# Attention logits of a hybrid decoder layer: two heads in two halves of the matrix array, or one head at a time in the whole of it; and two loads moved

## The chip, the core and the metric

The kernel runs on one core of a Trainium2 chip. A core has five engines that run their own instruction streams in order and wait for each other by semaphores: TensorE (PE in the profile; its weight loads are PEld), VectorE (DVE), ScalarE (ACT), GpSimd (POOL) and SyncE (SP), which here only issues DMAs. The metric is the device time of one execution in microseconds; lower is better.

## What is computed

One decoder layer on 256 tokens of width 1024, all in float32. The input is projected by one matrix `w_in`; three token mixers run on the columns; their outputs are gated, merged, projected by `w_out`, normalized (LN1), and passed through a feed-forward part with a second gate from a side input `p`, and normalized again. Cut to what the change touches:

```python
sc    = einsum('bqhd,bsd->bqhs', iq, ik) * 64**-0.5        # indexer: 8 heads of 64, one key head
index = einsum('bqh,bqhs->bqs', iw, relu(sc))              # its top 64 keys are those of mixer A
logits_A = einsum('bqhd,bkd->bqhk', q, k_shared)*s + bias  # branch A: 6 heads, one key head
logits_B = einsum('bqhd,bqjhd->bqhj', q_g, k_slot)*s + bias # dilated: 4 slots x 3 groups of queries
logits_C = q @ k.T * s + bias                              # block-sparse: 6 heads, own keys
merged = sum(sigmoid(x @ Wg_b) * (o_b @ P_b) for b in 'ABC')
x = LN(alpha * x + merged @ w_out)                         # LN1, with row vectors ln1_g and ln1_b
x = LN(alpha * x + relu(x @ w_up)**2 @ w_down + sigmoid(x @ w_ple_gate) * (p @ w_ple))
```

## The kernel before

**Numbers in two parts.** Every float32 operand of a matmul is split into a high part (a rounded copy, made by ACT) and a low part (what the rounding left, made by DVE and, for early weights, POOL). A product of two such operands takes three matmuls, high by high, high by low and low by high (`prod`, L133); low by low is dropped.

**Weights.** `Weights` (L50) holds a list of units, each up to 128 x 1024. For each it issues a load on SP into one of five `raw` buffers (L71), a cast on ACT (L75) and a subtraction on DVE or DVE and POOL (L79) into one of five pairs `whi`, `wlo`. `get(i, ahead)` emits the splits up to four units past the one wanted. `W.after` names instructions behind which the next splits are held.

**The order of the work.** A planner with a model of the machine orders the instructions of each engine before the run; on the chip each engine then keeps that order. `high_priority` moves instructions up in it, `issue_after` holds one behind another, and `keep_in_program_order` pins matmuls to each other.

**Projections.** `feat(f)` (L257) computes one tile of 128 features by 256 tokens (two heads of 64) into one of three `mm` banks of PSUM with 24 matmuls of 256 columns. The first four tiles, the indexer's queries, are computed together (L403 to L408). `fill("g")` computes a tile of the gates in the same way, and `fill("c")` a tile of the branch products; they lie between the attention steps and keep PE supplied.

**Logits.** `q_pair` (L214) splits a query tile: plane 0 is its high part, plane 1 its low part, both heads above each other on 128 partitions. `k_pair` (L222) does it for keys; with two arguments it writes the same 64 rows into both halves (the indexer's key kI and branch A's key kA). `logits(q, k)` (L264) takes one query tile and gives the two heads' logits in two PSUM banks: for each block of 128 queries three products, each product for head 1 and for head 0, so 12 matmuls. Each contracts over 64 partitions, that is, uses one half of the array's rows; six have 128 columns and six have 256. There are 16 calls: 4 for the indexer (L425), 6 for the dilated pairs (`slots`, L356), 3 for the block-sparse branch (L474) and 3 for branch A (L489). DVE adds the bias to the result and takes the row extreme; ACT takes the exponential; `attend` (L308) transposes the probabilities on PE, splits them and multiplies by the values.

**Merge, `w_out`, LN1.** `merge` (L561) gates and sums the branches. `outp` multiplies by `w_out` into four banks; its last four steps go bank by bank (`finish`, L547), and `ln1` (L630) follows each bank: add the residual `PL` (L634), statistics (L611 to L618), scale and shift by the row vectors `rows1` (L623, L625), transpose on PE (L644), split (L646, L647). `PL` and `rows1`, 1 MB each, are loaded by ACT's queue behind the sixth `muls` (L601 to L603). `finish` emits splits of units ahead before it emits `ln1`: the two of `w_ple`, and the first two of `w_ple_gate` (called wpg0 and wpg1 here). L660 multiplies the side input, split in `ph` and `pl` (L464 to L467), by `w_ple`.

**The rest.** The `w_ple_gate` product, 32 tiles of `w_up` (L693, L695) and `w_down`, partly in a scheme with seven products in place of eight, follow; the change does not touch them.

Of the kernel before, what the change touches and what calls it, by code (L numbers as in the profile page):

```python
# [11 lines left out]
F32 = mybir.dt.float32  # L12
# [37 lines left out]
class Weights:  # L50


    def __init__(self, tc, raw, part):
        self.tc, self.nc = tc, tc.nc
        self.raw, self.part = raw, part
        self.units, self.done, self.parts, self.after = [], 0, {}, ()

    def add(self, src, n, hi=None, lo=None, stage=None, by="v", urgent=0):
        i = len(self.units)
# [3 lines left out]
    def _split(self, i):  # L63
        nc = self.nc
        src, n, hi, lo, r, by, _ = self.units[i]
        if callable(src):
            r = src()
        else:
            if r is None:
                r = self.raw.tile([128, 1024], F32, name="raw", tag="raw")[:, :n]  # L70
            nc.sync.dma_start(r, src)  # L71
        if hi is None:
            hi = self.part.tile([128, 1024], F32R, name="whi", tag="whi")[:, :n]
            lo = self.part.tile([128, 1024], F32R, name="wlo", tag="wlo")[:, :n]
        nc.scalar.copy(hi, r)  # L75
        cut = ((nc.vector, slice(None)),) if by == "v" else (
            (nc.vector, slice(0, by * n // 1024)), (nc.gpsimd, slice(by * n // 1024, n)))
        for e, c in cut:
            low = e.tensor_tensor(lo[:, c], r[:, c], hi[:, c].bitcast(F32), op=ALU.subtract)  # L79
            if e is nc.gpsimd:  # L80
                self.pool = low.ins
        self.parts[i] = (hi, lo)
# [13 lines left out]
def hybrid_layer(ctx: ExitStack, tc: tile.TileContext, x0, xn, pT, wqk, wva, wvb, wg, wbc, wba,  # L96
# [56 lines left out]
    pm = mid.enter_context(tc.tile_pool(name="pm", bufs=1))  # L153
    one = ctx.enter_context(ExitStack())
    right = lambda n, b: one.enter_context(tc.tile_pool(name=n, bufs=b, side="right"))
    p1, k1, kp = (right(n, b) for n, b in (("p1", 1), ("k1", 2), ("kp", 3)))

    xh = p1.tile([128, KT, S], F32R, name="xh")
    xl = p1.tile([128, KT, S], F32R, name="xl")
# [13 lines left out]
    for t in TASKS:  # L173
# [8 lines left out]
        else:  # L182
            u_q.append([add(wqk[int(t) - FIRST], 1024)])

    def toeplitz(h0, step):
        t = tp.tile([128, 3, 256], F32, name="T", tag="T")
        for i in range(3):
            nc.sync.dma_start(t[:, i], bass.AP(
                tensor=tabd.tensor,
                offset=tabd.offset + (h0 + i * step) * COPIES * N_U + 127,  # L190
                ap=[[N_U - 16, 8], [N_U - 1, 16], [1, 256]]))
        return t


# [19 lines left out]
    def q_pair(ps, scale=-0.125):  # L214

        q = qpool.tile([128, 2, S], F32R, name="q", tag="q")
        last[0] = act.mul(q[:, 0], ps, scale).ins
        low[0] = dve.scalar_tensor_tensor(q[:, 1], ps, scale, q[:, 0].bitcast(F32),
                                          op0=ALU.mult, op1=ALU.subtract).ins
        return q  # L220

    def k_pair(a, b=None):  # L222

# [79 lines left out]
            dve.tensor_tensor(V[:, b, h0:h0 + heads, DH:128], src,  # L303
                              V[:, b, h0:h0 + heads, 0:DH].bitcast(F32), op=ALU.subtract)

    n_pt = [0]

    def attend(P, vh, o, h):  # L308

        pt = pts[n_pt[0] % 2]  # L310
        n_pt[0] += 1
        t = next(ps_t)
        for c in range(3):
            pe.transpose(t[:, 128 * c:128 * c + 128], P[:, 128 * c:128 * c + 128], ident)  # L314
        act.copy(pt[:, 0], t[:, 0:384])
        dve.tensor_tensor(pt[:, 1], t[:, 0:384], pt[:, 0].bitcast(F32), op=ALU.subtract)
        v = next(ps_v).rearrange("p (a s) -> p a s", a=2)
        pe.matmul(v, lhsT=V[:, 0, vh], rhs=pt[:, :, 0:256], start=True, stop=False)  # L318
        pe.matmul(v[:, :, 128:256], lhsT=V[:, 1, vh], rhs=pt[:, :, 256:384], start=False,
                  stop=True)  # L320
        x = wk2.tile([64, 2, S], F32, name="ov", tag="ov")
        act.copy(x, v[64:128])
        dve.tensor_tensor(x, v[0:64], x, op=ALU.add)
        dve.tensor_tensor(o[64 * h:64 * h + 64], x[:, 0], x[:, 1], op=ALU.add)
# [26 lines left out]
    def slots(qs, k, Ts, vh, o):  # L351

        es = [wk2.tile([128, 3, 384], F32, name="eb", tag="eb") for _ in range(2)]
        mxs = [sm.tile([128, 2, 3], F32, name="mxb", tag="mxb") for _ in range(2)]
        for g in range(3):
            s = logits(qs[g], k)  # L356
            for h in range(2):
                for b, t in enumerate((Ts[h][:, g, 128:256], Ts[h][:, g, :])):
                    dve.tensor_tensor_reduce(es[h][:, g, QC[b]], s[h][:, QC[b]], t, op0=ALU.add,
                                             op1=ALU.min, scale=1.0, scalar=-GONE,  # L360
                                             accum_out=mxs[h][:, b, g:g + 1])
        for h in range(2):
# [23 lines left out]
    with ExitStack() as begin:  # L386
# [17 lines left out]
        for k in range(KT):  # L404
            for i, (w, x) in enumerate(((sh, xh), (sh, xl), (sl, xh))):
                for f in range(FIRST):
                    pe.matmul(first[f], lhsT=w[:, k, 128 * f:128 * f + 128], rhs=x[:, k],  # L407
                              start=k == i == 0, stop=k == KT - 1 and i == 2)  # L408
        iq = [q_pair(ps, 0.125) for ps in first]
    tp, wk, wk2, sm = (right(n, b) for n, b in (("tp", 3), ("wk", 3), ("wk2", 2), ("sm", 6)))  # L410
    with tc.issue_after(low[0]):
        dve.tensor_tensor(tab, gone, tab, op=ALU.subtract)
# [9 lines left out]

    values(u_va, 328, 0, 5, True)
    for j in range(4):
        s = logits(iq[j], kI)  # L425
        r = wk2.tile([128, 768], F32, name="ri", tag="eb")
        r = r.rearrange("p (h k) -> p h k", h=2)
        for h in range(2):
# [20 lines left out]

    for j in range(2):  # L450
        ps = feat(5 + 4 * j)
        k = k_pair(ps)
        fill("g")
        qs = []
        for g in range(3):
            qs.append(q_pair(feat(6 + 4 * j + g)))
            if g:
                fill("g")
        o = opair()
# [1 line left out]
        slots(qs, k, Ts, 1 + 2 * j, o)  # L461
        pair_out(o, 3 + j)
        fill("g")
    pr = wk2.tile([128, 2, S], F32, name="pr", tag="eb")  # L464
    nc.sync.dma_start(pr, pT)
    act.copy(ph, pr)
    dve.tensor_tensor(pl, pr, ph.bitcast(F32), op=ALU.subtract)  # L467
    values(u_vb, 384, 5, 6, False)
    fill("g")
    for j in range(3):  # L470
# [14 lines left out]
        pass  # L485
    T = None
    for j in range(3):
        q = q_pair(feat(19 + j))
        s = logits(q, kA)  # L489
        o = opair()  # L490
        for h in range(2):
            n = 2 * j + h
# [33 lines left out]
    class Wide:  # L526
# [17 lines left out]
                for c in range(len(self.cut[b])):  # L544
                    self.go(k, b, c)

        def finish(self, ks, done, spare):  # L547

            for k in ks:
                self.ws[k] = W.get(self.units[k], min(AHEAD, ks[-1] - k + spare))  # L550
            for b in range(2):
                for c in range(len(self.cut[b])):
                    for k in ks:
# [40 lines left out]
    x1 = p3.tile([128, 2, KT, 2, 128], F32R, name="x1")  # L594
    rows1 = p3.tile([128, 2, D], F32, name="rows", tag="rows")

    def row_load(t, i):
        act.dma_start(t, lnrow[i:i + 2].rearrange("r d -> (r d)").partition_broadcast(128)
                      .rearrange("p (r d) -> p r d", r=2))

    with tc.issue_after(muls[5]):  # L601
        act.dma_start(PL, xn)
        row_load(rows1, 0)  # L603

    st = {}

# [41 lines left out]
        if b == 1:  # L648
            W.after = (i0.ins, i1.ins)

    outp.finish((4, 5, 6, 7), ln1, 5)


    wp = [W.get(u, 0) for u in u_ple]
# [309 lines left out]
```

## Time and profile before

| what | value |
|---|---|
| median of 3 runs | 435.42 us (434.95 to 435.57) |
| the profiled execution, its own time | 437.98 us |
| its span, first to last instruction | 436.2 us |
| mean granted TensorE clock in it | 0.994 |
| DMA | 86.39 MB, mean 198 GB/s |

The profile is of one execution. The time of an execution holds some 1.8 us outside the span. Busy time of an engine counts its instructions' durations, overlaps once. Matmuls are pipelined: the profile shows each with a duration of some 0.28 us, but the next one starts about 0.12 us later, so what PE spends on one is read from start to start. In a timeline, a row holds the start in us, the time in us that it covers, engine, line, operation, what is written and read, shapes, the count of instructions merged into it, and in brackets an idle time before it and what ended it. The chain of waits follows the last instruction back to what released it.

### The profile page before, as it was taken

Reading aid. Unit: us, or ns where it says so; the run is one execution under the profiler, and the core shown is the slowest. Engines: PE = TensorE matmul, PEld = TensorE weight load, DVE = VectorE, ACT = ScalarE, POOL = GpSimd, SP = SyncE. Lnnn points to the kernel's source line nnn. Section 1 sums busy time; section 2 is a strip of 40 time slices with the busy share of each in tenths; the row PEclk is TensorE's granted clock in tenths of the full one; section 3 lists DMA queues with packets and bytes.
Section 4 is the critical chain, followed back from the end, with each engine's and each line's share of the span. In section 5 each row is a group of like instructions: output and inputs, shape, how many; then the busy total and the mean of one; then the engine's idle time right before and its main releaser. Section 6 shows DMA issues by size and latency. Waiting matters only on the chain.

```text
span 436.2 us, 7669 instructions
## 1 busy us (share of the span) xinstructions
PE 425.1 (97%) x2799; PEld 386.0 (88%) x2799; DVE 350.5 (80%) x625; ACT 276.2 (63%) x490; POOL 105.4 (24%) x98
## 2 busy tenths in 40 slices
PE   8999999999999999999998999999999999999993
PEld 8999999999999999999886888888888888888882
DVE  5978987577476577879957779999988897998984
ACT  6775375586787777756524567788887855665500
POOL 2563355395434566400000000000100000000001
PEclk9999999999999999999999999999999999999997
DMA  8797756457654436455960875656795377758411
GB/s 298 291 326 234 230 173 191 150 189 250 183 151 145 128 109 187 144 192 178 400 246 0 288 237 185 187 180 203 277 268 187 115 207 269 200 192 278 155 41 57
DMA packets 27690, 86.39 MB, mean 198 GB/s; under 512 B 2884, under 2 KB 6892, under 8 KB 27268
## 3 DMA queue, kind: packets, MB, share of 16 engines
q1 hardware_dynamic: 25872, 79.54, 55.1%
q0 software_dynamic: 640, 2.17, 2.9%
q10 hardware_dynamic: 1140, 4.19, 2.6%
q8 instruction: 22, 0.36, 0.3%
q14 instruction: 16, 0.13, 0.1%
HBM read 83.99 MB, written 1.90 MB: 197 GB/s over the span
## 4 chain that ended last, share of the span: by engine, by line
PE 88%; DVE 5%; issue 3%; DMA 2%; POOL 0%; POOLq 0%; ACT 0%; DVEq 0%; ACTq 0%
PE mm L136 40%; PE b L136 18%; PE mm L693 13%; PE mm L695 7%; PE b L274 3%; PE b L407 3%; DMA raw<-in_wpg_dram 2%; PE b L314 1%; PE b L318 1%; DVE hT L79 1%; DVE st L611 1%; DVE Y L625 1%; PE b L131 1%; DVE G L570 1%; DVE Y L634 1%
## 5 line engine op out<-in xcount | busy, mean ns | idle before, releaser
L79 DVE TENSOR_TENSOR wlo<-raw,whi 128x1024 fp32r<-128x1024 f32 (+5 forms) x146 | 157.5, 1092 | 41.9 <-ACT whi L75 37.9
L75 ACT CAST whi<-raw 128x1024 fp32r<-128x1024 f32 (+3 forms) x146 | 146.1, 1011 | 48.8 <-PE b L136 11.7
L79 POOL TENSOR_TENSOR wlo<-raw,whi 128x384 fp32r<-128x384 f32 (+3 forms) x58 | 78.8, 1367 | 82.6 <-ACT whi L75 73.6
L136 PE MATMUL mm<-xl,whi 128*128 128x256 f32 x336 | 95.7, 285 | 0.0
L136 PE MATMUL mm<-xh,whi 128*128 128x256 f32 x336 | 95.3, 284 | 0.0
L136 PE MATMUL mm<-xh,wlo 128*128 128x256 f32 x336 | 95.0, 283 | 0.0
L136 PEld LDWEIGHTS mm<-xl,whi 128*128 128x128 f32 x336 | 63.3, 188 | 1.0
L693 PE MATMUL mm<-x,whi 128*128 128x512 f32 x256 | 64.1, 392 | 0.0
L136 PEld LDWEIGHTS mm<-xh,whi 128*128 128x128 f32 x336 | 63.3, 188 | 0.7
L136 PEld LDWEIGHTS mm<-xh,wlo 128*128 128x128 f32 x336 | 63.3, 188 | 0.3
L693 PEld LDWEIGHTS mm<-x,whi 128*128 128x128 f32 x256 | 46.1, 189 | 8.3
L136 PE MATMUL b<-whi,hT 128*128 128x512 f32 (+2 forms) x164 | 51.8, 381 | 0.0
L695 PEld LDWEIGHTS mm<-x,wlo 128*128 128x128 f32 x256 | 34.9, 190 | 2.5
L741 POOL DMA_DIRECT2D rows<-in_wdq_dram x4 | 3.6, 972 | 135.3 <-DVE wlo L79 81.9
L695 PE MATMUL mm<-x,wlo 128*128 128x256 f32 x256 | 35.7, 282 | 0.0
L136 PEld LDWEIGHTS b<-whi,hT 128*128 128x128 f32 x164 | 30.5, 188 | 5.8
L136 PE MATMUL b<-wlo,hT 128*128 128x512 f32 (+2 forms) x82 | 31.2, 381 | 0.0
L618 POOL TENSOR_TENSOR rs<-rs,half 128x1 f32<-128x1 f32 x4 | 4.1, 1031 | 103.3 <-DVE rs L617 103.3
L698 DVE TENSOR_REDUCE r<-mm 128x256 f32<-128x512 f32 x32 | 22.0, 688 | 4.9 <-PE mm L695 4.9
L136 PE MATMUL mm<-op,whi 128*128 128x256 f32 x128 | 23.6, 281 | 0.0
L136 PE MATMUL b<-whi,x 128*128 128x512 f32 x64 | 20.4, 394 | 0.0
L241 ACT ACTIVATE G<-mm 128x256 f32<-128x256 f32 x24 | 9.2, 381 | 17.4 <-PE mm L136 17.3
(162 smaller groups left out, 740.0 us busy)
## 6 DMA issues: line engine op xcount, KB each, us to landing
raw<-in_wup_dram SPq DMA_DIRECT2D x32, 512.0 KB
raw<-in_wg_dram SPq DMA_DIRECT2D x24, 512.0 KB
raw<-in_wqk_dram SPq DMA_DIRECT2D x18, 512.0 KB
raw<-in_wdn_dram SPq DMA_DIRECT2D x16, 512.0 KB
raw<-in_wdq_dram SPq DMA_DIRECT2D x12, 512.0 KB
raw<-in_wout_dram SPq DMA_DIRECT2D x8, 512.0 KB
raw<-in_wpg_dram SPq DMA_DIRECT2D x8, 512.0 KB
T<-tabd SPq DMA_DIRECT2D x24, 128.0 KB
```

The lines of the kernel that those rows point to most:

```text
L75: nc.scalar.copy(hi, r)
L79: low = e.tensor_tensor(lo[:, c], r[:, c], hi[:, c].bitcast(F32), op=ALU.subtract)
L131: pe.transpose(t[:, 0:128], ident, ident)
L136: m = pe.matmul(ps, lhsT=a[x], rhs=b[y], start=first and i == 0, stop=last and i == 2)
L241: act.activation(G[:, n_g[0]], ps, AF.Tanh, scale=0.5)
L274: m = pe.matmul(ss[h][:, QC[b]], lhsT=q[d, x, c], rhs=k[d, y, 0:128 * (b + 1)], start=i == 0, stop=i == 2)
L314: pe.transpose(t[:, 128 * c:128 * c + 128], P[:, 128 * c:128 * c + 128], ident)
L318: pe.matmul(v, lhsT=V[:, 0, vh], rhs=pt[:, :, 0:256], start=True, stop=False)
L407: pe.matmul(first[f], lhsT=w[:, k, 128 * f:128 * f + 128], rhs=x[:, k], start=k == i == 0, stop=k == KT - 1 and i == 2)
L693: pe.matmul(ps, lhsT=hi[:, cs[k]], rhs=x1[:, :, k], start=k == 0, stop=False)
L695: pe.matmul(ps[:, :, 0], lhsT=lo[:, cs[k]], rhs=x1[:, :, k, 0], start=False, stop=k == KT - 1)
L698: dve.tensor_reduce(r, ps.rearrange("p b a t -> p b t a"), axis=AX.X, op=ALU.add)
```

## The change

Logits of the indexer, the dilated pairs and branch A go to a new function `whole`; the block-sparse branch stays with `logits`. Queries for `whole` are made by `q_stack`: for head 0, plane 0 holds its high part in partitions 0 to 63 and its low part in 64 to 127; for head 1, plane 1 holds its high part in 64 to 127 and its low part in 0 to 63. Keys have to stand in both halves, so the dilated pairs' keys are written twice (`k_pair` with two arguments, once for each head); kI and kA were so already. A matmul of 128 rows with the key's high parts then gives high by high plus low by high, and one with its low parts gives high by low plus low by low. That is 8 matmuls of 128 rows a call, four of 128 columns and four of 256.

The load of the side input and that of the first row vectors move. `pr` gets the place of the last two gate tiles in `G` in place of a buffer that the softmax uses; its load is held behind the last bias load of the second dilated pair, its split behind the last split of probabilities. `rows1` goes from ACT's queue to SP's, behind the load of wpg1.

```diff
-    p1, k1, kp = (right(n, b) for n, b in (("p1", 1), ("k1", 2), ("kp", 3)))
+    p1, k1, kp = (right(n, b) for n, b in (("p1", 1), ("k1", 4), ("kp", 2)))
...
+    def q_stack(ps, scale=-0.125):
+
+        q = qpool.tile([128, 2, S], F32R, name="q", tag="q")
+        for h in range(2):
+            a, b = (slice(64 * i, 64 * i + 64) for i in (h, 1 - h))
+            last[0] = act.mul(q[a, h], ps[a], scale).ins
+            low[0] = dve.scalar_tensor_tensor(q[b, h], ps[a], scale, q[a, h].bitcast(F32),
+                                              op0=ALU.mult, op1=ALU.subtract).ins
+        return q
+
+    def whole(q, ks):
+
+        ss = [None, None]
+        with tc.high_priority(offset=500):
+            for h in range(2):
+                ss[h] = next(ps_s)[:, 0:384]
+                for b in range(2):
+                    for y in range(2):
+                        m = pe.matmul(ss[h][:, QC[b]], lhsT=q[:, h, b * 128:(b + 1) * 128],
+                                      rhs=ks[h][:, y, 0:128 * (b + 1)], start=y == 0, stop=y == 1)
+                        if b or y:
+                            tc.keep_in_program_order(m)
+        return ss
...
-            s = logits(qs[g], k)
+            s = whole(qs[g], k)
...
-        iq = [q_pair(ps, 0.125) for ps in first]
+        iq = [q_stack(ps, 0.125) for ps in first]
...
-        s = logits(iq[j], kI)
+        s = whole(iq[j], (kI, kI))
...
-        k = k_pair(ps)
+        k = [k_pair(ps[i:i + 64], ps[i:i + 64]) for i in (0, 64)]
...
-            qs.append(q_pair(feat(6 + 4 * j + g)))
+            qs.append(q_stack(feat(6 + 4 * j + g)))
...
-    pr = wk2.tile([128, 2, S], F32, name="pr", tag="eb")
-    nc.sync.dma_start(pr, pT)
-    act.copy(ph, pr)
-    dve.tensor_tensor(pl, pr, ph.bitcast(F32), op=ALU.subtract)
+    pr = G[:, 22:24]
+    with tc.issue_after(table[0]):
+        nc.sync.dma_start(pr, pT)
+    with tc.issue_after(cast[0]), tc.issue_after(cast[1]):
+        act.copy(ph, pr)
+        dve.tensor_tensor(pl, pr, ph.bitcast(F32), op=ALU.subtract)
...
-        q = q_pair(feat(19 + j))
-        s = logits(q, kA)
+        q = q_stack(feat(19 + j))
+        s = whole(q, (kA, kA))
...
-        row_load(rows1, 0)
...
-    outp.finish((4, 5, 6, 7), ln1, 5)
+    def rows_load():
+        with tc.issue_after(W.loads[u_pg[1]]):
+            row_load(rows1, 0, nc.sync)
+
+    outp.finish((4, 5, 6, 7), ln1, 5, rows_load)
```

`finish` calls `rows_load` between its splits and its matmuls; `row_load` takes the queue as an argument; `table`, `cast` and `W.loads` only note the instructions that others are held behind.

More of the change, by code (lines that the diff above doesn't have):

```diff
@@ L55, in __init__ @@
         self.raw, self.part = raw, part
-        self.units, self.done, self.parts, self.after = [], 0, {}, ()
+        self.units, self.done, self.parts, self.after, self.loads = [], 0, {}, (), {}
     def add(self, src, n, hi=None, lo=None, stage=None, by="v", urgent=0):
@@ L70, in _split @@
                 r = self.raw.tile([128, 1024], F32, name="raw", tag="raw")[:, :n]
-            nc.sync.dma_start(r, src)
+            self.loads[i] = nc.sync.dma_start(r, src).ins
         if hi is None:
@@ L183, in hybrid_layer @@
             u_q.append([add(wqk[int(t) - FIRST], 1024)])
+    table = [None]
     def toeplitz(h0, step):
@@ L187, in toeplitz @@
         for i in range(3):
-            nc.sync.dma_start(t[:, i], bass.AP(
+            table[0] = nc.sync.dma_start(t[:, i], bass.AP(
                 tensor=tabd.tensor,
                 offset=tabd.offset + (h0 + i * step) * COPIES * N_U + 127,
-                ap=[[N_U - 16, 8], [N_U - 1, 16], [1, 256]]))
+                ap=[[N_U - 16, 8], [N_U - 1, 16], [1, 256]])).ins
         return t
@@ L304, in v_out @@
                               V[:, b, h0:h0 + heads, 0:DH].bitcast(F32), op=ALU.subtract)
-    n_pt = [0]
+    n_pt, cast = [0], [None, None]
     def attend(P, vh, o, h):
@@ L314, in attend @@
             pe.transpose(t[:, 128 * c:128 * c + 128], P[:, 128 * c:128 * c + 128], ident)
-        act.copy(pt[:, 0], t[:, 0:384])
-        dve.tensor_tensor(pt[:, 1], t[:, 0:384], pt[:, 0].bitcast(F32), op=ALU.subtract)
+        cast[0] = act.copy(pt[:, 0], t[:, 0:384]).ins
+        cast[1] = dve.tensor_tensor(pt[:, 1], t[:, 0:384], pt[:, 0].bitcast(F32),
+                                    op=ALU.subtract).ins
         v = next(ps_v).rearrange("p (a s) -> p a s", a=2)
@@ L545, in step, with finish @@
                     self.go(k, b, c)
-        def finish(self, ks, done, spare):
+        def finish(self, ks, done, spare, loaded):
             for k in ks:
                 self.ws[k] = W.get(self.units[k], min(AHEAD, ks[-1] - k + spare))
+            loaded()
             for b in range(2):
@@ L595, in hybrid_layer, with row_load @@
     rows1 = p3.tile([128, 2, D], F32, name="rows", tag="rows")
-    def row_load(t, i):
-        act.dma_start(t, lnrow[i:i + 2].rearrange("r d -> (r d)").partition_broadcast(128)
+    def row_load(t, i, by=act):
+        by.dma_start(t, lnrow[i:i + 2].rearrange("r d -> (r d)").partition_broadcast(128)
                       .rearrange("p (r d) -> p r d", r=2))
```

## The prediction, made before the changed kernel was run

> **What bounds the kernel now.** I read the page first, for the engines' shares and the chain of waits.
>
> ```profile
> PE 425.1 (97%) x2799; PEld 386.0 (88%) x2799; DVE 350.5 (80%) x625; ACT 276.2 (63%) x490; POOL 105.4 (24%) x98
> PE 88%; DVE 5%; issue 3%; DMA 2%; POOL 0%; POOLq 0%; ACT 0%; DVEq 0%; ACTq 0%
> ```
>
> PE is busy for 97% and carries 88% of the chain. The rest of the chain, a few per cent of DVE, DMA and issue, must lie in one or a few places, and a saving of PE's work counts only outside these. So I asked for the busy time of each engine by stretches: from the end of the first projection to the end of `w_out`, LN1, and from there to the last product.
>
> ```profile
> 17.00:225.00 208.00, 208.00 (x1669) 198.87 (x1668) 156.54 (x375) 135.57 (x278) 92.03 (x76) 1.00 0.62 203
> 225.00:237.00 12.00, 10.23 (x51) 7.78 (x50) 11.20 (x21) 4.04 (x7) 2.01 (x2) 1.00 0.11 44
> 237.00:420.00 183.00, 183.00 (x929) 156.23 (x928) 162.06 (x193) 123.84 (x182) 3.57 (x4) 1.00 0.65 204
> ```
>
> The columns are the stretch, its length, then PE, PEld, DVE, ACT and POOL, the granted clock and the DMA. PE is busy without a break in the first and third stretch, at full clock, with DVE at 75% and 89%. It idles only in LN1. So there are two ways to gain: shorter PE work before 225 us, where each PE microsecond is one of the kernel, or the closing of the holes in LN1. All logits lie in the first stretch.
>
> **The logits on PE.** The timeline of PE around one call:
>
> ```profile
> 29.92 0.28 PE L136 MATMUL mm<-xh,wlo 128*128 128x256 f32 x1
> 30.13 0.95 PE L274 MATMUL b<-k,q 64*128 64x128 f32 x12
> 31.01 0.39 PE L136 MATMUL mm<-xl,whi 128*128 128x256 f32 x1
> 31.23 0.28 PE L136 MATMUL mm<-xh,whi 128*128 128x256 f32 x1
> ...
> 33.00 0.28 PE L136 MATMUL mm<-xh,whi 128*128 128x256 f32 x1
> ```
>
> From the start at 31.23 to that at 33.00 there are 15 steps, so a matmul of 256 columns costs 1.77 / 15 = 0.118 us. Between 29.92 and 31.23 lie the 12 logit matmuls and two ordinary ones: 1.31 - 2 x 0.118 = 1.07 us for the call. The first step into it (0.21), and the two out of it (the call covers to 31.01, then 0.22 to the next), are each longer than 0.118: PE loses time when it turns from whole-array to half-array matmuls and back.
>
> What the new matmuls cost is bounded by 256 columns at 0.118 from above. For 128 columns with all 128 rows there is a row at the very end, in the last columns of `w_down`:
>
> ```profile
> 426.50 0.27 PE L136 MATMUL b<-wlo,hT 128*128 128x128 f32 x1
> ...
> 427.72 0.83 PE L136 MATMUL b<-x,hT 128*128 128x128 f32 x6
> ```
>
> Eleven start from the first of these to the second: 1.22 / 11 = 0.111 us each. So half the columns save almost nothing, and a call of `whole` costs 4 x 0.111 + 4 x 0.118 = 0.92 us, if it joins its neighbours without a break. That it does is read from the transposes, other short work of the whole array between the projections, in the chain of waits:
>
> ```profile
> 93.93 0.11 PE b L314
> 94.04 0.12 PE mm L136
> ```
>
> A transpose of 128 columns takes 0.11 even alone between two projection matmuls. So 1.07 - 0.92 = 0.15 a call, and 13 calls give 2.0 us. One call is now cut in two by three other matmuls, and turns twice more; these are its last eight:
>
> ```profile
> 25.86 0.73 PE L274 MATMUL b<-k,q 64*128 64x128 f32 x8
> ```
>
> The twelve matmuls in six pairs, two heads at once, would take 3 x 0.111 + 3 x 0.118 = 0.69 without any turn, so entering and leaving cost 1.07 - 0.69 = 0.38 us together. The cut call pays this twice; that adds 0.4 to the saving. Sum for the logits: **-2.4 us**.
>
> The Trainium skill's page "TensorEngine Tiling (Array Packing)", section "Theoretical Speedup", gives up to twofold speed to contractions of at most 64 rows. By that rule alone the old form, 0.69 in six pairs, would beat the new one, 0.92, by 0.23 a call, and the change would cost 3.0 us; the same page, under "Key Properties", says that a change of tiling mode drains TensorE, without a price, and this trace's 0.38 us a call puts the price above that advantage.
>
> **What the split costs on ACT and DVE.**
>
> ```profile
> L218 DVE SCALAR_TENSOR_TENSOR q<-mm,q 128x256 fp32r<-128x256 f32 x12 | 5.0, 418 | 1.6 <-ACT q L217 1.4
> L229 DVE TENSOR_TENSOR k<-mm,k 128x256 fp32r<-128x256 f32 (+1 forms) x9 | 3.8, 417 | 0.3
> L217 ACT ACTIVATE q<-mm 128x256 fp32r<-128x256 f32 x12 | 4.6, 384 | 8.4 <-PE mm L136 8.2
> ```
>
> The group L229 holds keys of 128 and of 64 partitions and means the same as L218, which has 128 alone, so half the partitions save nothing; I take that for ACT too. `q_stack` has two of each where `q_pair` had one: 13 more. The dilated keys go from one of each to four: 6 more. That is 19 x 0.418 = 7.9 us on DVE and 19 x 0.384 = 7.3 us on ACT, all in a stretch where DVE has 208 - 156.5 = 51 us free and ACT 72. I cost them at nothing. What covers them is the distance between a query's split and its logits, filled by gate tiles. The tightest place is the first dilated pair, with the top-k on DVE:
>
> ```profile
> 40.00:60.00 20.00, 20.00 (x180) 19.19 (x179) 19.33 (x86) 8.59 (x15) 7.08 (x6) 1.00 0.72 212
> 53.05 0.40 DVE L218 SCALAR_TENSOR_TENSOR q<-mm,q 128x256 fp32r<-128x256 f32 x1
> 55.01 0.95 PE L274 MATMUL b<-k,q 64*128 64x128 f32 x12
> ```
>
> Here the low part is done at 53.45 and PE needs it at 55.01: 1.56 us in hand, and one more pair of instructions takes 0.38 + 0.42 = 0.80. DVE has only 0.67 us free in these 20 us, and the pair's six extra instructions are 2.5; but the top-k, which is wanted only by branch A, two branches later, can give way. The cost here lies between 0 and 2.5 - 0.67 = 1.8 us; I take 0, since the margin is twice the added latency, and keep 1.8 for the range. The `mm` bank is held longer by the same 0.8, against the two tiles of 2.8 us (24 x 0.118) that pass before its next turn.
>
> **The two loads.** PE, ACT and DVE in LN1:
>
> ```profile
> 228.75 0.39 PE L136 MATMUL mm<-whi,pl 128*128 128x512 f32 x1
> 229.59 0.66 PE L644 MATMUL b<-ident,Y 128*128 128x128 f32 x4 [0.45 <-DVE Y L625]
> ...
> 232.15 0.40 PE L136 MATMUL b<-wlo,x 128*128 128x512 f32 x1
> 233.87 0.33 PE L644 MATMUL b<-ident,Y 128*128 128x128 f32 x1 [1.32 <-DVE Y L625]
> ```
> ```profile
> 212.39 0.36 ACTq L598 DMA_DIRECT2D rows<-in_lnrow_dram  x1
> ...
> 215.25 1.05 ACT L75 CAST whi<-raw 128x1024 fp32r<-128x1024 f32 x1 [0.20 <-DMA raw<-in_wpg_dram]
> 221.48 1.05 ACT L75 CAST whi<-raw 128x1024 fp32r<-128x1024 f32 x1 [5.17 <-DMA raw<-in_wpg_dram]
> ```
> ```profile
> 214.17 3.49 DVE L79 TENSOR_TENSOR wlo<-raw,whi 128x1024 fp32r<-128x1024 f32 x3
> 222.56 1.23 DVE L79 TENSOR_TENSOR wlo<-raw,whi 128x1024 fp32r<-128x1024 f32 x1 [4.90 <-ACT whi L75]
> 223.70 1.28 DVE L634 SCALAR_TENSOR_TENSOR Y<-PL,b 128x512 f32<-128x512 f32 x2
> ```
> ```profile
> 214.00:222.00 8.00, 8.00 (x37) 6.62 (x36) 3.66 (x4) 2.62 (x3) 0.00 (x0) 1.00 1.02 409
> ```
>
> PE waits twice for the transposes: 0.84 and 1.72 us from start to start where about 0.23 is ordinary for 512 columns (2 x 0.118), 0.61 + 1.49 = 2.1 us lost. DVE is late because wpg1's subtraction stands ahead of LN1 in its queue and its data are late: DVE stands still for 4.9 us while the DMA engines are full (share 1.02, 409 GB/s), and in that time they carry the 1 MB of row vectors too, which was issued at 212.39. Behind wpg1, these no longer share with it: 1 MB at 409 GB/s is 2.6 us, the least by which wpg1 comes earlier; the most is DVE's whole 4.9. The two holes need 2.1 in sum, so both ends close them: **-2.1 us**. What is late next is PE itself, by its last bank:
>
> ```profile
> 229.45 0.68 DVE L634 SCALAR_TENSOR_TENSOR Y<-PL,b 128x512 f32<-128x512 f32 x1
> ```
>
> DVE takes that bank at 229.45, 4.4 us before the transpose at 233.87; `w_out`'s matmuls end at 225, so LN1 has 4.4 us to come earlier, twice what the holes need, and the `w_ple` product (24 x 0.23 = 5.4 us) runs meanwhile.
>
> ```profile
> 227.46 1.41 DVE L623 SCALAR_TENSOR_TENSOR Y<-Y,mv,rows 128x512 f32<-128x512 f32 x2
> ```
>
> The rows are wanted here, 3.8 us after LN1's first add. Wpg1 and the rows move as many bytes together as now, so the later of them lands no later than wpg1 did, by 221.5; even with LN1 earlier by 4.4 the scaling comes at 223.1. On SP the issue takes 0.36 us, and the loads of later `w_ple_gate` units stand behind it; their splits are held until the end of LN1, far behind 228. ACT's queue loses the same 0.36.
>
> The move of the side input's load and split changes when ACT and DVE wait, not PE, which has no gap there; its first use is in LN1. SP issues it earlier, behind the bias loads, at the same count of DMAs. I cost it at nothing; without the gate tiles that hide it, its cost would be one ACT and one DVE instruction of about a microsecond together, in either direction.
>
> **Sum.** -2.4 - 2.1 = -4.5 against the profiled execution's 437.98: 433.5. The median stands at 435.42, 0.9942 of it, so **430.9 us**.
>
> **Rivals.**
> Only the logits gain: another wait takes the place of wpg1's in LN1, such as the row vectors, now behind it, or a late DMA engine. For it: DMA is full to 222. Against: the bytes ahead of both are the same as now. 437.98 - 2.4 = 435.6, or 433.0 by the median.
> Only LN1 gains: PE's longer steps belong to the short call, not to the array's halves, or the extra splits eat the saving. Against: the transposes above join without a break. If the 0.38 stays with the call, the new call costs 0.38 + 0.92 = 1.30, 0.23 more than now, which is 13 x 0.23 - 0.4 = +2.6, and with LN1's -2.1 the sum is +0.5: 435.9 by the median. If the extra splits alone eat the 2.4, it is 433.3. By the tiling page's rule the result would be of the same kind as the former, +3.0 - 2.1.
> Slower: late stacks. In front of each of the 13 calls, the second head's ACT and DVE instructions queue behind one weight cast and one subtraction (1.01 and 1.09 us, the groups below), so the stack is complete 0.38 + 0.42 + 1.01 + 1.09 = 2.9 us later than now. Of this 1.56 us is covered, and PE waits 1.3 us a call: +17, less 4.5, about 448 by the median. It decides from 4.5 / 13 = 0.35 us a call, an added 1.9 us of latency.
>
> ```profile
> L79 DVE TENSOR_TENSOR wlo<-raw,whi 128x1024 fp32r<-128x1024 f32 (+5 forms) x146 | 157.5, 1092 | 41.9 <-ACT whi L75 37.9
> L75 ACT CAST whi<-raw 128x1024 fp32r<-128x1024 f32 (+3 forms) x146 | 146.1, 1011 | 48.8 <-PE b L136 11.7
> ```
>
> Against it: there are gate tiles to run meanwhile, and PE's order is planned with the longer splits known. That `whole` does not do what it says I don't see: eight matmuls replace twelve.
>
> **How the numbers follow.** Both gains, 0.64; only the logits, 0.14; only LN1 with the splits eating the rest, 0.09; no real change (the call keeps its break), 0.06; late stacks, 0.07. A measurement of this kernel can tell about 0.2%, 0.9 us, from no change. The first three are faster, the fourth the same, the last slower. The range runs from 429.6 (0.1 us more for each call) to 433.4, which holds the first three cases and the 1.8 us of the tight place.
>
> **What would show it.** Right: L274 left with 3 calls (36 matmuls), 104 of the new line; the step into and out of `whole` at 0.11 to 0.12; a call at about 0.92. The hole before the transposes gone, DVE's wait before wpg1's subtraction under 2.5 us, and DVE and ACT with 19 more instructions each in all. Wrong: an idle PE before `whole` or its neighbours between 17 and 222 us, 0.2 us steps at its ends, or PE waiting for L625 as before.

## The result and the profile after

| kernel | median | runs | lowest to highest |
|---|---|---|---|
| before | 435.24 us | 4 | 434.95 to 435.57 |
| after | 440.01 us | 4 | 439.51 to 440.13 |

Before has one execution more here than in the table ahead of the prediction.

The ratio after / before is 1.0099, 95% interval 1.0087 to 1.0112: slower by 1%, or 4.8 us, where 4.5 us less had been forecast. The profiled execution of after took 440.13 us (span 438.3 us, clock 0.991), as the median does. One execution among the experiments, the profiled one of e12_loads_held, took 851.96 us; the median given there counts it, the ratio does not, and its profile is not used.

The page of after, in the lines that answer to those shown of before (busy time by engine, and the chain of waits):

```profile
PE 424.7 (97%) x2747; PEld 389.0 (89%) x2747; DVE 366.0 (83%) x644; ACT 282.6 (64%) x509; POOL 100.7 (23%) x98
PE 81%; DVE 9%; issue 4%; DMA 3%; SPq 1%; ACT 1%; POOL 0%; POOLq 0%; DVEq 0%
```

DVE and ACT have 19 instructions more each, as counted (625 to 644, 490 to 509), and PE 52 fewer. PE's busy time hardly fell, but its share of the chain went from 88% to 81%. The stretches between the first projection and the second dilated pair (columns as before: PE, PEld, DVE, ACT, POOL, clock, DMA), after:

```profile
17.00:40.00 23.00, 22.35 (x174) 21.79 (x173) 21.11 (x40) 16.39 (x35) 10.94 (x11) 1.00 0.79 260
40.00:60.00 20.00, 17.49 (x133) 17.11 (x133) 19.27 (x70) 8.46 (x15) 5.23 (x6) 0.91 0.64 200
60.00:80.00 20.00, 18.78 (x159) 18.53 (x158) 16.76 (x47) 14.01 (x30) 11.24 (x10) 1.00 0.65 192
```

Before, PE was busy in all of 17 to 225 us. Now it idles in each of the three, most in the middle one, and there the granted clock is 0.91. What PE waited for between 17 and 222 us (total, times, longest):

```profile
PE mm L136 <- DVE k L255: 1.7, 2, 1.2
PE b L242 <- DVE q L230: 1.3, 1, 1.3
PE b L345 <- DVE pt L342: 1.2, 1, 1.2
PE b L242 <- ACT ri L456: 0.2, 1, 0.2
```

All but the last end with a split on DVE: the low part of a key (L255), of a query (L230), of the probabilities (L342). Counted from start to start against an ordinary step, the five idles cost 0.61 us at 28.3, 0.37 at 34.5, 1.46 at 43.4, 1.37 at 45.4 and 1.38 at 74.2, together 5.2 us.

**The account.** From the first matmul of the second group of projections (17.3 us before, 17.1 after) to the first of `w_out` (203.07 and 207.73), PE takes 185.8 us in before and 190.7 in after: +4.9, which is the whole difference of the medians. From there to the last matmul of `w_out` it is 21.6 in both, and from `w_up`'s first matmul to PE's last one 171.9 in both. What went on in between, in LN1, comes further down.

The two middle idles, and what came after them, in the timeline of PE in after:

```profile
43.37 0.28 PE L136 MATMUL mm<-xl,whi 128*128 128x256 f32 x1
44.95 0.73 PE L242 MATMUL b<-k,q 128*128 128x128 f32 x4 [1.30 <-DVE q L230]
46.89 0.36 PE L136 MATMUL mm<-xh,whi 128*128 128x256 f32 x1 [1.21 <-DVE k L255]
...
47.79 0.39 PE L136 MATMUL mm<-xh,wlo 128*128 128x256 f32 x1
...
51.17 0.31 PE L136 MATMUL mm<-xl,whi 128*128 128x256 f32 x1
```

From 47.79 to 51.17 there are 16 steps of 256 columns in 3.38 us, 0.21 each where 0.118 is ordinary. The windows of after around that place say why:

```profile
43.50:47.80 4.30, 1.79 (x14) 1.47 (x13) 4.11 (x14) 2.06 (x4) 1.19 (x2) 1.00 1.06 293
47.80:51.20 3.40, 3.40 (x19) 3.40 (x18) 3.24 (x12) 0.38 (x1) 0.00 (x0) 0.50 0.72 248
```

PE was busy for 1.8 of 4.3 us, and then its clock was at half for 3.4 us. This costs 3.38 - 16 x 0.118 = 1.5 us. So of the +4.9, 5.2 are idles and 1.5 are half clock. That leaves -1.8 for the rest of PE's work; an independent figure for it comes with e9_held.

**Where DVE was.** The timeline of DVE in after, up to the split for which PE waits at 44.95; L466 is the top-k, L79 a weight's subtraction, L255 a key's low part, L230 a query's:

```profile
41.21 0.61 DVE L466 MAX8 m<-idx 128x8 f32<-128x128 f32 x2
...
41.99 0.81 DVE L79 TENSOR_TENSOR wlo<-raw,whi 128x640 fp32r<-128x640 f32 x1
...
43.43 0.42 DVE L255 TENSOR_TENSOR k<-mm,k 64x256 fp32r<-64x256 f32 x1
43.78 0.41 DVE L466 MAX8 m<-idx 128x8 f32<-128x256 f32 x1
...
44.48 0.42 DVE L230 SCALAR_TENSOR_TENSOR q<-mm,q 64x256 fp32r<-64x256 f32 x1
...
46.31 0.43 DVE L255 TENSOR_TENSOR k<-mm,k 64x256 fp32r<-64x256 f32 x1
```

ACT's side of the same time:

```profile
35.22 0.36 ACT L254 CAST k<-mm 64x256 fp32r<-64x256 f32 x1
37.42 0.36 ACT L254 CAST k<-mm 64x256 fp32r<-64x256 f32 x1 [0.42 <-DVE k L255]
40.35 0.37 ACT L254 CAST k<-mm 64x256 fp32r<-64x256 f32 x1 [0.83 <-DVE k L255]
40.85 0.38 ACT L229 ACTIVATE q<-mm 64x256 fp32r<-64x256 f32 x1
43.89 0.37 ACT L254 CAST k<-mm 64x256 fp32r<-64x256 f32 x1 [1.72 <-DVE k L255]
```

Two things are to be seen. The query's high part was done at 41.23, and its low part began at 44.48: it stood 3.25 us in DVE's queue, behind the top-k, one subtraction and a key. And the dilated key's eight instructions go to and fro: ACT's second cast waits for DVE's first subtraction, and so on, although each pair writes a half of its own. They read the same `mm` bank, and it is the bank that they have in common: ACT's third cast, at 40.35, writes another tile than DVE's second subtraction does, and waits for it all the same. At DVE's full queue one such round takes up to 3.5 us, so the bank that two instructions of 0.8 us together emptied before is held from 35.2 to 46.7, and the next tile's matmul at 46.89 waits for it.

That row was to be had in the trace of before, where `k_pair` with two arguments makes kI and kA (L228 ACT, L229 DVE): timelines of ACT and of DVE in before,

```profile
20.31 0.37 ACT L228 CAST k<-mm 64x256 fp32r<-64x256 f32 x1 [1.98 <-PE mm L136]
...
25.03 0.37 ACT L228 CAST k<-mm 64x256 fp32r<-64x256 f32 x1
```
```profile
21.19 0.41 DVE L229 TENSOR_TENSOR k<-mm,k 64x256 fp32r<-64x256 f32 x1
...
25.90 0.43 DVE L229 TENSOR_TENSOR k<-mm,k 64x256 fp32r<-64x256 f32 x1
```

Four and four, in turn, took 6.0 us (20.3 to 26.3) there, not 4 x 0.8 = 3.2. A weight's cast or subtraction stands between every two of them in both queues, so the 6.0 is the price of the turns together with the queues, not of the turns alone.

### The profile page after: what moved, and what is told of

Read it like the earlier page. It is cut to its first block, busy times and chain, and to the rows that moved or that the text cites. A ratio compares the mean times of both kernels' runs of the same rounds, so it can differ in the third digit from the quotient of the medians.

```text
span 438.3 us, 7613 instructions
## 1 busy us (share of the span) xinstructions
PE 424.7 (97%) x2747; PEld 389.0 (89%) x2747; DVE 366.0 (83%) x644; ACT 282.6 (64%) x509; POOL 100.7 (23%) x98
## 4 chain that ended last, share of the span: by engine, by line
PE 81%; DVE 9%; issue 4%; DMA 3%; SPq 1%; ACT 1%; POOL 0%; POOLq 0%; DVEq 0%
PE mm L136 33%; PE b L136 23%; PE mm L726 13%; PE mm L728 7%; DVE wlo L79 3%; DMA raw<-in_wqk_dram 2%; PE b L242 2%; DVE idx L459 1%; PE b L340 1%; DMA raw<-in_wvb_dram 1%; DVE idx L467 1%; PE b L345 1%; SPq L422 1%; DVE q L230 1%; DVE m L466 1%
## 5 line engine op out<-in xcount | busy, mean ns | idle before, releaser
L79 DVE TENSOR_TENSOR wlo<-raw,whi 128x1024 fp32r<-128x1024 f32 (+5 forms) x146 | 160.9, 1114 | 30.5 <-ACT whi L75 29.5
L79 POOL TENSOR_TENSOR wlo<-raw,whi 128x384 fp32r<-128x384 f32 (+3 forms) x58 | 72.8, 1261 | 93.8 <-ACT whi L75 82.1
L136 PE MATMUL b<-whi,x 128*128 128x512 f32 x64 | 20.3, 394 | 0.0
L136 PEld LDWEIGHTS mm<-op,whi 128*128 128x128 f32 x128 | 19.7, 188 | 0.1
```

What stands on the lines that cost most here:

```text
L136: m = pe.matmul(ps, lhsT=a[x], rhs=b[y], start=first and i == 0, stop=last and i == 2)
```

## The experiments

The theory: the added splits find DVE's queue full, since the top-k fills it from 41 to 63 us; PE's idles follow from this, and from the handing to and fro. The rivals: the loads' move costs the time; the new matmuls cost it; ACT and DVE have too much work whatever the order. Each ratio is to runs of before on the same chip, with its 95% interval.

**e1_loads: only the loads' move.** All logits as before (`logits`, `q_pair`, one pair of instructions for a dilated key).

> The kernel before with the two moved loads alone; all logits as before. By the prediction's step (holes in LN1 closed) it is 2.1 to 2.4 us faster than before: about 432.9. Rival: the profiled execution of before was 2.7 us above its median, so the late wpg1 may belong to that execution; then ordinary runs have little hole to close, and this kernel takes 435.2, no change.

Measured: 435.09 us, 0.999 (0.9979 to 1.0), no idle of PE in the stretch, which takes 185.7 us as in before. The loads' move costs nothing and brings nothing that can be told. LN1's transposes join without a gap, but see the next.

**e0_before: before once more, with a profile.**

> The kernel before once more, for a second profile of it. The moved loads alone changed nothing in time (435.09 against 435.47), though their profile shows LN1 2.4 us shorter than the profile of before. If the holes in LN1 belonged to the one profiled execution (437.98, 2.7 over its median), this profile has w_out's last matmul to w_up's first at about 29.3 us and not 31.7; if the holes are ordinary, 31.7 again, and something else in the moved loads took the gain back.

Measured: 435.38 us, 1.0001 (0.9988 to 1.0013); the profiled execution took 435.23. From `w_out`'s last matmul to `w_up`'s first it takes 29.3 us, as after (29.3) and e1_loads (29.3), where before's first profile had 31.7. The hole in LN1 was that execution's own. The cast of wpg1 in ACT's timeline, of e0_before and then of after:

```profile
218.50 1.05 ACT L75 CAST whi<-raw 128x1024 fp32r<-128x1024 f32 x1 [2.76 <-DMA raw<-in_wpg_dram]
```
```profile
222.78 1.05 ACT L75 CAST whi<-raw 128x1024 fp32r<-128x1024 f32 x1 [1.13 <-DMA raw<-in_wpg_dram]
```

ACT waits 2.76 us for wpg1 in e0_before, against 5.17 in the profile that was predicted from, and 1.13 after. So the move does bring wpg1 earlier, but in an ordinary execution nothing on PE had waited for it.

**e2_group: the splits in another order.** Both of ACT's, then both of DVE's, in `q_stack`; the same with four and four in the dilated keys. The work is the same.

```diff
+        ab = [[slice(64 * i, 64 * i + 64) for i in (h, 1 - h)] for h in range(2)]
-        for h in range(2):
-            a, b = (slice(64 * i, 64 * i + 64) for i in (h, 1 - h))
+        for h, (a, b) in enumerate(ab):
             last[0] = act.mul(q[a, h], ps[a], scale).ins
+        for h, (a, b) in enumerate(ab):
             low[0] = dve.scalar_tensor_tensor(q[b, h], ps[a], scale, q[a, h].bitcast(F32),
...
```

> The changed kernel with the same splits in another order: in each stacked query both ACT instructions first, then both DVE instructions; in the doubled keys four, then four. Count and durations on ACT and DVE are the same. Theory 1 (handover: instructions of ACT and DVE on one PSUM bank wait for each other in turn, so the old order is a chain of four or eight steps, each behind other work in its queue): the PE stalls of 5.3 us between 28 and 76 us and the 1.9 us at half clock go, 440.0 - 7.2 = 432.8. Theory 2 (load: DVE simply has too much work there): no change, 440.

Measured: 437.47 us, 1.0042 (1.0027 to 1.0056). This lies between the two forecasts. The idles fall from 5.2 to 3.75 us, the half clock is gone: 2.5 of the 4.8 us, so the order was about half of the loss. ACT's four casts of a dilated key stand in one row of its timeline in e2_group,

```profile
34.18 1.51 ACT L484 CAST k<-mm 64x256 fp32r<-64x256 f32 x4
```

where they ran from 35.22 to 44.26 in after.

**e3_pool: DVE relieved of part of the weights.** `DV = 640` becomes `DV = 448`: POOL takes more of each split weight's columns.

> The changed kernel with DV = 448 in place of 640: POOL takes 576 of the 1024 columns of each early low part in place of 384, so DVE has 0.2 us less for each of 58 units, some 3 us less up to 50 us and 11 us in all. Theory 2 (load): the stalls go or halve, 433 to 436. Theory 1 (handover): the steps queue behind somewhat shorter work, so only a small gain, 438 to 440.

Measured: 442.12 us, 1.0144 (1.0125 to 1.0163): slower still, outside both forecasts, idles 6.5 us. Between 17 and 80 us DVE's busy time hardly fell (57.1 to 56.7 us; between 40 and 60 it even rose from 19.27 to 19.47), POOL's rose from 27.4 to 35.6, and PE now waited for ACT as well. So the edit did not relieve DVE, and the run neither carried the theory nor broke it. The traces show where the relief went: a DVE subtraction that begins while POOL is at work ends a fixed time behind POOL's instruction (last section), and POOL's subtractions became longer (1.37 to 1.73 us on average). Undisturbed, DVE's part takes 0.61 us in place of 0.81, which is 8.4 us over the 42 units cut at 640 before; their mean fell only from 1.04 to 0.95 us, 4.0 us in all.

**e4_topk: the top-k emitted later.** In `feat`, `if f > 4:` becomes `if f > 8:`.

> The changed kernel with the eight rounds of the top-k moved from the feature tiles 5 to 12 to the tiles 9 to 16: DVE is free of four rounds, about 5.6 us, in the first dilated pair, where two of the three stalls lie. Theory 2 (load): the stalls at 43 to 47 us (2.8 us and the half clock of 1.9 us) go, 435 to 436; the one at 74 us may grow. Theory 1 (handover): the weight subtractions of 0.8 us stay in the queue, so at most half of it goes, 438 to 440.

Measured: 440.53 us, 1.0104 (1.0075 to 1.0132), the same four rows of waits as after. The first MAX8 (the top-k's first instruction) stands at 41.4 us, as before the edit (41.2): the planner took it as soon as its input was there, from both places of emission. The run tested nothing but showed that.

**e5_a, e6_idx_a, e7_dil: one group of calls alone.** e5_a has only branch A in `whole`, e6_idx_a the indexer and branch A, with grouped splits (kI's and kA's too), e7_dil the dilated pairs alone, as in the change. The loads are as in the change in each.

> The moved loads and, of the logits, branch A alone in the whole array; its keys were doubled before already, so each of three queries has one more instruction on ACT and on DVE, late in the stretch, with nothing on PE waiting close behind. If the array's saving is real and only the splits' place is at fault (theory 1 and 2 alike), 3 x 0.15 = 0.45 us under the kernel with the loads alone: 434.6. If the saving itself is not real, 435.1.

> Indexer and branch A in the whole array, the dilated pairs as before; the splits grouped (ACT's first, then DVE's), those of the indexer's and branch A's doubled keys too. Theory 1 (handover): the stall of 0.6 to 1.2 us at 28 us goes too, and 7 calls save 7 x 0.15 + 0.4 = 1.4: 433.7 against 435.1 for the loads alone. Theory 2 (load): four more DVE instructions between 19 and 23 us push the stall at 28 us as in the changed kernel: 434.5 to 435.

> The dilated pairs alone as in the change (alternating splits, keys written twice), indexer and branch A as before, with the moved loads. If the loss sits in the dilated pairs' own chain of handovers, their stalls of 2.8 us at 43 to 47 us with the half clock of 1.9, and the 1.4 at 74 us, stay: 435.1 - 0.9 + 6.1 = 440. If the indexer's added work in front (theory 2, a backlog on DVE) is needed for it, 436 to 437.

| | median us | ratio | stretch us | idles us |
|---|---|---|---|---|
| e5_a | 435.10 | 0.999 (0.9976 to 1.0004) | 185.2 | 0 |
| e6_idx_a | 437.45 | 1.0041 (1.0028 to 1.0053) | 187.2 | 2.4 |
| e7_dil | 438.32 | 1.0068 (1.0043 to 1.0093) | 188.3 | 2.9 |

e5_a's total is that of the forecast without a saving, but the 0.45 us of the other forecast is less than these totals can tell, and its stretch is shorter. e6_idx_a came out above both of its forecasts, and e7_dil between its two. The profiled executions of the last two took 436.70 and 437.41 us, less than their medians, so their stretches and idles are rather low.

Branch A's three calls shorten the stretch by 0.55 us against 185.7 and wait for nothing; in the total it can't be told. In e6_idx_a the largest idle, 1.0 us at 43.1, stands before a call of the first dilated pair, which is made as before there: what PE waited for between 17 and 222 us in e6_idx_a (L301 is `logits`, L220 `q_pair`'s low part), and the stretch of that idle:

```profile
PE b L301 <- DVE q L220: 0.8, 1, 0.8
...
40.00:60.00 20.00, 18.67 (x167) 17.69 (x166) 19.96 (x80) 6.47 (x10) 5.05 (x5) 1.00 0.66 203
```

So DVE's backlog is passed on to calls that the change does not touch: it is the load on DVE, 19.96 of 20 us, and not the new call (e11_idx_a_held, below, is the test). e7_dil loses more, 2.1 us of it in one place, at 70.0, in front of the first pair's `attend`; there DVE's split stands behind a weight's subtraction of 1.67 us.

**e8_allgroup: e2_group, with kI's and kA's splits grouped too.**

> The changed kernel with every doubled split grouped: queries, dilated keys, and the indexer's and branch A's keys, which alternate in the kernel before too. Theory 1: against the grouped kernel without the last (437.5), the stall of 1.24 us at 28 us goes: 436.2, or 434.9 if the later waits follow from it. Theory 2: no change, 437.5.

Measured: 437.97 us, 1.005 (1.0032 to 1.0068), stretch 187.9, idles 3.5: no different from e2_group.

**e9_held: the change as it is, with the top-k held.** Its first instruction may not run before the first dilated pair's last split of probabilities.

```diff
-        if f > 4:
+        if f > 8:
             next(side, None)
...
-                dve.max(m8, idx[:, QC[b]])
+                with tc.issue_after(cast[1]):
+                    dve.max(m8, idx[:, QC[b]])
```

> The changed kernel with the top-k held behind the last split of probabilities of the first dilated pair (the try that only called it later left it in its old place on DVE). DVE loses some 11 us of work between 41 and 75 us. Theory 2 (load): PE's stalls of 2.8 us at 43 to 47 us and the half clock of 1.9 us go; those at 28 us (0.6) and perhaps 74 us (1.4) stay: 440.0 - 4.7 = 435.3. Theory 1 (handover alone): the chain of eight steps still waits in turn for casts on ACT and subtractions on DVE; at least half of it stays, 437.7 or more.

Measured: 434.78 us, 0.9981 (0.9972 to 0.9991): 5.2 us of the change's loss gone. The top-k begins at 74.3 us. The stretch from 40 to 60, and DVE around the split that had been late, in e9_held:

```profile
40.00:60.00 20.00, 20.00 (x172) 19.98 (x171) 14.98 (x46) 10.66 (x22) 8.36 (x7) 1.00 0.79 245
```
```profile
43.69 0.43 DVE L255 TENSOR_TENSOR k<-mm,k 64x256 fp32r<-64x256 f32 x1 [0.43 <-ACT k L254]
44.15 0.42 DVE L230 SCALAR_TENSOR_TENSOR q<-mm,q 64x256 fp32r<-64x256 f32 x1
```

PE has no gap there, the clock stays at 1.00, and here DVE waits for ACT. What is left of idles in the stretch is 1.1 us: 0.76 at 29.0 (a bank held by kA's low part) and 0.37 at 35.3. The idle of after at 74.2 us is gone too, though the top-k had ended 11 us before it there; by which way the hold removes that one is not shown.

**e12_loads_held: the control.** e1_loads with the same hold.

> Control: the loads and the held top-k, all logits as before. If the top-k's place matters only because the extra splits leave DVE no time (load), there is no PE stall to remove here and the time is that of before, 435.1 to 435.6. If holding the top-k is a gain by itself, it is 434.8 or less, and the held versions owe their gain to it and not to the array.

Measured: 435.51 us, 0.999 (0.9977 to 1.0003). The hold by itself brings nothing that can be told; it only takes away what the added splits cost.

**e10_held_group, e11_idx_a_held: e2_group and e6_idx_a with the hold.**

> The changed kernel with the dilated keys and the queries grouped and the top-k held. If both causes add (an order of handovers, and a DVE with no free time), the stalls between 45 and 75 us go and only that at 28 us stays: 437.5 - 2.5 = 435.0, at best 433.8. If load does not matter once the handovers are gone, 437.5.

> Indexer and branch A in the whole array, grouped, dilated pairs as before, and the top-k held. Its PE stalls (1.0, 0.6, 0.2 us between 43 and 56 us, all waits for DVE) stood in a part that the change does not touch there. Theory 2 (load, a backlog on DVE passed on from the indexer): they go, 437.45 - 1.8 - some small ones = 435 to 435.6 or lower, at best 433.7. Theory 1 alone: 437.5.

Measured: 434.63 us, 0.9984 (0.9967 to 1.0002), and 435.40, 0.9995 (0.9983 to 1.0006). With the queue free the order of the splits no longer tells (e9_held against e10_held_group). In e11_idx_a_held the idles of e6_idx_a between 43 and 56 us, in front of calls that the change does not touch, are gone. The idle that stays is the indexer's: 1.05 us at 29.5 in e10_held_group, and 0.86 at 24.3 with 0.31 at 34.6 in e11_idx_a_held.

**e13_dil_a_held, e14_best: is there a version that beats both?** The former is e10_held_group with the indexer as before (`q_pair`, `logits`), so that nothing is added between 17 and 35 us. The latter is e10_held_group with kI's and kA's splits grouped and moved up.

> Dilated pairs and branch A in the whole array, grouped, top-k held, indexer as before. Nothing is added on DVE before 31 us, so the stall at 28 to 29 us is gone; 9 calls save 9 x 0.15 = 1.4 us: 435.4 - 1.4 = 434.0. If some stall of the held versions is not due to the indexer's added splits, 434.6 or more.

> All 13 calls in the whole array, grouped, top-k held, and the splits of the indexer's and branch A's keys grouped and moved up in the planned order, ahead of weights. If the last stall of 1.0 us at 29 us is the key's low part standing behind weights on DVE, it goes: 434.6 - 1.0 = 433.6. If the four instructions added for the indexer's queries alone fill DVE there, the stall only moves: 434.6.

Measured: e13_dil_a_held 434.17 us, 0.9962 (0.9947 to 0.9977); e14_best 434.40, 0.9963 (0.9947 to 0.9978). Both beat before, by 0.4%. e13_dil_a_held has no idle of PE between 17 and 222 us; two of its stretches:

```profile
17.00:40.00 23.00, 23.00 (x192) 21.60 (x192) 20.03 (x37) 15.77 (x32) 13.15 (x11) 1.00 0.83 280
40.00:60.00 20.00, 20.00 (x172) 20.00 (x171) 13.48 (x43) 11.03 (x22) 7.00 (x6) 1.00 0.72 225
```

Its stretch takes 184.3 us, 1.5 less than before's, with nine calls in `whole`: 0.16 a call. In e14_best the idle mostly moved, to 1.25 us at 24.6, where `whole` itself waits for kI's low part.

Of the rivals, the loads' move falls with e1_loads, and a cost of the new matmuls with e13_dil_a_held, which keeps nine of the calls and is shorter by them. Too much work for DVE whatever the order is half true: the order is worth half of the loss while the top-k is there (e2_group), and with the top-k held the same added work costs about 1 us of idle (e9_held).

## Why the prediction was wrong

**What bounds the kernel: right for PE, wrong for LN1.** PE without a break from 17 to 225 us is what e0_before shows again.

**The logits on PE: right, kind and size.** 3 calls are left with `logits` and 104 matmuls stand in the new line. The timeline of PE in after where nothing waits (branch A):

```profile
87.17 0.28 PE L136 MATMUL mm<-xh,wlo 128*128 128x256 f32 x1
87.29 0.62 PE L242 MATMUL b<-k,q 128*128 128x128 f32 x4
87.75 0.28 PE L136 MATMUL mm<-xl,whi 128*128 128x256 f32 x1
```

The step in is 0.12 us, and one head's four matmuls take 87.75 - 87.29 = 0.46, so a call takes 0.92, without a break at either end. Foreseen for 13 calls were 2.4 us. Without idles, the stretch of 185.8 is 1.9 us shorter in e9_held (185.0 - 1.1 = 183.9 against 185.8) and 2.4 in e10_held_group (184.5 - 1.05 = 183.4). So the rival by which the call keeps its break fell: whole-array calls are shorter here, with the turn priced in. With it fell, as a forecast for this kernel, the up to twofold speed that the Trainium skill's page "TensorEngine Tiling (Array Packing)", section "Theoretical Speedup", gives to short contractions. That the page's own drain (section "Key Properties") is the reason agrees with the 0.38 us a call, but no run measured a drain by itself.

**"I cost them at nothing": the step that failed.** The extra splits on ACT and DVE cost 5.2 us of idle and 1.5 us of half clock in place of 0, with 1.8 kept for the range. Their count and their durations were right (19, at some 0.42 us on DVE); three statements under it were not. The prediction's own sign of being wrong, an idle PE before `whole` or its neighbours between 17 and 222 us, is what came.
- "The top-k ... can give way": it did not. The planner lays it from 41.2 to 62.5 us, where before had it from 43.0 to 59.1, and e4_topk shows that it goes there from a later place of emission too. e9_held makes it give way, and 5.2 us come back; e12_loads_held shows that the hold has no gain of its own. This is shown.
- "1.56 us in hand", against 0.80 added: the margin was that of one instruction at the place where it stood. The split's wait in DVE's queue was not in the working, though DVE's 19.33 of 20 us stood quoted beside it. After the change a query's low part waited 3.25 us.
- "The `mm` bank is held longer by the same 0.8": a key's bank was held for 11.5 us, as four and four instructions wait for each other in turn, each behind other work in its queue. e2_group shows that this order is about half of the loss while the queue is full; e9_held against e10_held_group shows that it is nothing that can be told once the queue is free. The Trainium skill's page "PSUM — Partial Sum Buffer", section "PSUM bank collisions raise a hardware error", says that two engines may not use the same bank and quadrant of partitions at once, two reads included, but may use different quadrants of a bank. The waits here fit the first part; the two heads lie in different quadrants and waited all the same, which by the second part would not be needed. No run here tried it.

**The clock: not in the sum at all.** 1.5 us follow from the two idles of 43 to 47 us. e4_topk has the same two idles and the same half clock behind them (0.91 between 40 and 60 us), and it is gone wherever those idles are shorter (e2_group, e3_pool, e9_held). What half clock costs apart from the idles before it was read from the rows, not tested by itself.

**The hole in LN1, -2.1: wrong.** The hole was in the one execution that the sum was made against, and in no other profile, e0_before's of the same kernel among them. The hint stood in the prediction's own last step: 437.98 against a median of 435.42 is 2.6 us too long, and the hole was 2.1. Multiplying by 0.9942 took the hole off once, and the sum took it off a second time. What the prediction said of the bytes is borne out (wpg1's wait is shorter), but the time to be had was 0. The 0.36 us for an issue on SP was a row of ACT's queue; on SP it took 0.43 in after, which changes nothing.

**The rivals.** Late stacks, at 7 in 100, is the one that came nearest: splits queued on DVE, PE waiting in front of them. Its place and price were off: 17 us were foreseen in front of all 13 calls, and 5.2 were found, in front of two calls, two `mm` tiles and one `attend`, all between 28 and 76 us. Behind that nothing waited.

**With the terms put right**: -1.9 for PE's work, as e9_held shows it, +5.2 and +1.5 make +4.8, where +4.8 was measured. The idles and the half clock are from after's own trace, so this tests the -1.9 and not them.

What stays open: what the hold does for the idle at 74.2 us; what the last idle at 24 to 30 us needs (moving kI's and kA's splits up only moved it); and an idle of 0.25 to 1.4 us at 7 to 10 us, in the first product, in some profiles (e1_loads, e4_topk, e5_a, e8_allgroup, e9_held, e10_held_group, e14_best) and not in others, which ACT's first splits end where the trace names a cause.

## What to carry to other kernels

Work added to an engine that is nearly full in a stretch is not costed by its free time or by the margin of one instruction: ask how long such an instruction stands in that engine's queue there, and how many handovers between engines hang on one buffer. Work of no urgency on that engine gives way only if something holds it back; look where the planner puts it, since here one hold was worth 5 us to the change and nothing without it. And before a hole is entered as a gain, set the profiled execution beside the median: if it is longer by just the hole, the hole is not there in the others.

## What the runs showed of the hardware

- **Half clock after two short idles.** PE idled 1.30 and 1.21 us, was busy for 1.64 of the 3.41 us up to 47.80, and then ran at 0.50 for 3.41 us. That stretch in the windows of after:

```profile
44.39:47.80 3.41, 1.64 (x12) 1.47 (x13) 3.22 (x11) 1.69 (x3) 1.01 (x1) 1.00 1.07 309
```

  The clock of after rises at 6.85 us and falls at 47.81, 12 x 3.413 later. On the same grid in e7_dil, from its rise at 5.71, a single idle of 1.98 us left PE busy for 1.72 us between 70.57 and 73.98, and the clock stayed at 1.00. So the longest idle does not decide here; the busy share of a stretch (0.48 and 0.50) would fit both, but they lie close and no run set out to test it. The Trainium skill's page "TensorE: Matmul & The Clock Gate", section "What's actually happening", has a window of 3413 ns, whose length agrees, and names an idle window as the cause; here PE was busy for almost half of it.
- **One late DMA engine.** In before's first profile, 15 of the 16 DMA engines had delivered wpg1 by 219.3 us, the last one at 221.4. The cast and all behind it waited for that one, and LN1 took 31.7 us in place of e0_before's 29.3.
- **A DVE subtraction that begins beside a POOL instruction waits for its end.** With 640 columns it takes 0.81 us in some places and up to 1.69 in others. DVE and POOL in after:

```profile
70.43 1.43 DVE L79 TENSOR_TENSOR wlo<-raw,whi 128x640 fp32r<-128x640 f32 x1 [0.64 <-POOL wlo L79]
...
73.45 1.69 DVE L79 TENSOR_TENSOR wlo<-raw,whi 128x640 fp32r<-128x640 f32 x1 [0.57 <-ACT whi L75]
```
```profile
70.18 1.00 POOL L398 TENSOR_TENSOR eb<-eb 128x384 f32<-128x384 f32 x1
...
73.44 1.02 POOL L79 TENSOR_TENSOR wlo<-raw,whi 128x384 fp32r<-128x384 f32 x1 [0.70 <-DMA T<-tabd]
```

  POOL's two end at 71.18 and 74.46, DVE's at 71.86 and 75.14, each 0.68 us later. Of the 42 such subtractions in after, 20 begin when POOL has 0.2 us or more of an instruction left; 19 of them end 0.68 us behind it, whatever it works on, and the other 23 take 0.81 to 0.83. In e3_pool, with 448 columns, the distance is 0.48. Lying side by side is not enough: where DVE began first it took its 0.81 to 0.83. No run isolated this, but it is the row to look for before DVE's work is costed by its mean duration. The idle at 74.2 us is behind such a subtraction, 0.88 us longer than it is alone.
